# Feed-forward activations of a decoder layer in one tile for the whole stage, with the 2x2 blocks turned

## Chip, cores and metric

One core of a Trainium2 chip (trn2) runs the whole layer in one launch. The metric is device time in microseconds, the time of the slowest core (here the only one), lower is better.

## What is computed

One post-norm decoder layer on 512 tokens of width 2048, in float32. Most of the reference does not matter here. The change lies in the feed-forward part, of which the first matrix product is this:

```python
x = layer_norm(DEEPNORM_ALPHA * x + mix, ln_mix_g, ln_mix_b)
f = jnp.square(jax.nn.relu(x @ w_ff1)) @ w_ff2        # w_ff1: 2048 x 8192, w_ff2: 8192 x 2048
x = layer_norm(DEEPNORM_ALPHA * x + f, ln_ff_g, ln_ff_b)
```

## The kernel before

**Precision.** Every float32 product is made of three matmuls: each operand is split into a high part (written by ScalarE, `wh`, `aH`, L87) and a rest (written by VectorE, `wl`, `aL`, L88), and high x high, high x rest and rest x high are added in PSUM.

**The first feed-forward product in units.** The 8192 hidden columns are taken as 16 groups of 512. Group 0 is computed plainly. Groups 1 to 15 are the units (`FUnit`). A unit is a 2x2 block product (tokens in two halves of 256, features in two halves of 1024, hidden columns in two halves of 256) made with seven products M1 to M7 instead of eight, in the order M1, M5, M6, M3, M7, M2, M4 (`ORDER`). Each product is two pieces (`FPiece`), so a unit is pieces 0 to 13, each 24 matmuls of 256 columns at L654. Its blocks are called by two digits, as "11" or "21". The activations `yH`, `yL` and their sums `ysH`, `ysL` stay on chip. The four weight blocks of a unit (`w1`, 1 MB each, tags handed from unit to unit) are loaded by SyncE's queue at L611: `give` at pieces 6, 7, 9 and 11 of a unit loads the next unit's blocks, in the order "11", "12", "22", "21", each into the buffer of a block that is used up.

**The order of the work is the program's own.** Ahead of piece i, `fill` issues the splits of piece i+2 (ScalarE, then VectorE; M1 and M5 pieces also add one weight block to another on VectorE, L615: for M1, "12" is added onto "11"), then `beside` issues the side work of piece i, then `mult` issues the matmuls of piece i. Three pairs of `wh`, `wl` buffers exist, so a split waits until the matmuls three pieces earlier are done. Every engine takes its instructions in program order. Counting on over the end of a unit, this text calls the next unit's pieces 0, 1, 2 and 3 also pieces 14, 15, 16 and 17.

**The results of a unit.** They are put into `R[g]`, a tile `hpR` of 2 halves x 8 slots x 256 tokens with one buffer (tag "R"). Slots 0 to 3 are the four output blocks. At piece 10 VectorE writes slot 2 (-M1-M6 as copied, less M5) and slot 3 (the copied -M5 less the bank of M1, L663), ScalarE applies the ReLU to both at piece 11 (L666), VectorE writes slot 0 at piece 12, ScalarE applies its ReLU at piece 13. Products M6, M7 and M4 are added in PSUM onto the bank of M1, and M4 is pieces 12 and 13: its first matmul can start only when slot 3's subtraction has read that bank. When the unit is over (`done`, in the next unit's piece 0), ScalarE writes slot 1 with the ReLU of the bank (L620) and squares slots 0 to 3 (L621).

**Sending them out.** In the next unit, for groups 0 to 13, VectorE forms slots 4 to 7 out of slots 0 to 3 at pieces 2 and 3 (`h_sums`, L548). At pieces 5 and 7 slots 1 to 7 of one half are split (`hpH`, L87 and L88) and sent to `h_parts` in DRAM by two transfers of 896 KB each on GpSimd's queue (L555). Slot 0 is not sent: the second product has no factor that is this block alone. Groups 14 and 15 send slots 0 to 3 instead (`h_rest`).

**Other work in the same stage.** On GpSimd's queue, `y_load` at piece 7 brings three 256 KB pieces, and `y_rows` at piece 11 makes two VectorE operations (L526, L527) and sends 256 KB (L531). After the 15 units the second product starts (L789), whose operands come back from `h_parts`.

```python
def h_rows(g):
    R[g] = L2["p"].tile([P, 2, 8, 256], F32, name="hpR", tag="R")
...
elif j == 10:
    h_rows(u.g)
    block(2, u2, v["M5"], OP.subtract)
    block(3, m5, v["M1"], OP.subtract)
```

A new tile on a tag with one buffer may be written when all that used the old tile is done. Inside one tile an instruction waits for the earlier ones whose data it overlaps.

Of the kernel before, what the change touches and what calls it, by code (L numbers as in the profile page):

```python
# [9 lines left out]
F32 = mybir.dt.float32  # L10
F32R = mybir.dt.float32r
I32 = mybir.dt.int32
AF = mybir.ActivationFunctionType
OP = mybir.AluOpType
PSUM = bass.MemoryType.PSUM

P = 128
# [51 lines left out]
def decoder_layer(ctx: ExitStack, tc: tile.TileContext, x, xt, positions, w_in, w_pool, pool_scale,  # L69
                  w_branch_attn, w_branch_pool, w_out, ln_mix_g, ln_mix_b, w_ff1, w_ff2,  # L70
                  ln_ff_g, ln_ff_b, consts, vectors, out, h_parts, h_rest, y_norm, y_parts):
    nc = tc.nc
# [13 lines left out]
    def split(dst_h, dst_l, src):  # L86
        nc.scalar.activation(dst_h, src, AF.Copy)  # L87
        nc.vector.tensor_tensor(dst_l, src, dst_h.bitcast(F32), op=OP.subtract)  # L88
# [348 lines left out]
    L2 = {}  # L437
# [16 lines left out]
    yH, yL = mH, mL  # L454
# [8 lines left out]


    yr, sums = {}, {}
    RAW = {"11": "t11", "12": "t10", "21": "t1", "22": "t12"}
    SUM = {"P1": ("t7", "t8"), "P2": ("t9", "t12"), "P4": ("t11", "t6")}

    def ln1_t(t0, j):
        half, k0 = t0 // 2, 2 * j % 8  # L470
        who = str(half + 1) + str(j // 4 + 1)
        if k0 == 0:
            yr[who] = L2["p"].tile([P, 8, 256], F32, name="yr", tag=RAW[who])
        p = PS.tile([P, 2, 2 * P], F32, name="sc" if j % 2 else "tp", bufs=1)
        for e in range(2):
            k = 2 * j + e
            for t in range(2):
                nc.tensor.transpose(p[:, e, t * P:(t + 1) * P], acc[t0 + t][:, k * P:(k + 1) * P], ident)
        y = yr[who][:, k0:k0 + 2]
        for e in range(2):  # L480
            k = 2 * j + e
            nc.scalar.activation(y[:, e], p[:, e], AF.Identity, bias=bcol[:, k:k + 1], scale=gcol[:, k:k + 1])
        c = slice(2 * j % 4, 2 * j % 4 + 2)
        t = slice(t0 * P, (t0 + 2) * P)
        split(yH[j // 2][:, c, t], yL[j // 2][:, c, t], y)

    def ln1_side(t0):
        return [lambda: ln1_norm(t0)] + [lambda j=j: ln1_t(t0, j) for j in range(8)]
# [4 lines left out]
    def y_sum(name, src):  # L493
        h = L2["p"].tile([P, 8, 256], F32R, name="ysH", tag=SUM[name][0])
        l = L2["p"].tile([P, 8, 256], F32R, name="ysL", tag=SUM[name][1])
        if name == "P2":
            nc.scalar.activation(h, yr[src], AF.Copy, scale=-1.0)
            nc.vector.scalar_tensor_tensor(l, yr[src], -1.0, h.bitcast(F32), op0=OP.mult, op1=OP.subtract)
        else:
            split(h, l, yr[src])  # L500
        sums[name] = (h, l)
# [8 lines left out]
    def y_p3():  # L510

        for c in range(2):
            split(yH[c][:, :, 256:], yL[c][:, :, 256:], yr["21"][:, 4 * c:4 * c + 4])


    def y_load(t, n):
        c = slice(n * 512, (n + 1) * 512)
        nc.gpsimd.dma_start(low["u"][:, 1], y_norm[t, :, c])
        nc.gpsimd.dma_start(low["g"][:, 0], bcast(ln_mix_g, c))
        nc.gpsimd.dma_start(low["g"][:, 1], bcast(ln_mix_b, c))  # L520

    def y_rows(t, n):
        c = slice(n * 512, (n + 1) * 512)
        v, g, b = low["u"][:, 1], low["g"][:, 0], low["g"][:, 1]
        stt = nc.vector.scalar_tensor_tensor
        stt(v, v, ALPHA, g, op0=OP.mult, op1=OP.mult)  # L526
        stt(v, b, ALPHA, v, op0=OP.mult, op1=OP.add)  # L527
        if t >= 2 and n % 2:
            nc.gpsimd.dma_start(g, y_parts[t - 2, :, c])
            return lambda: y_rest(t, c)  # L530
        nc.gpsimd.dma_start(y_parts[t, :, c], v)  # L531
# [11 lines left out]
    R = {}  # L543
# [25 lines left out]
        return {2: lambda: h_sums(g, slice(0, 2)), 3: lambda: h_sums(g, slice(2, 4)),  # L569
                5: lambda: h_parts_out(g, 0), 7: lambda: h_parts_out(g, 1)}  # L570

    def h_rows(g):
        R[g] = L2["p"].tile([P, 2, 8, 256], F32, name="hpR", tag="R")

    def ff1_evac(g):

        def f(b, p):
            if g not in R:
                h_rows(g)
            t = R[g][:, b % 2, 2 * (b // 2):2 * (b // 2) + 2]  # L580
            nc.scalar.activation(t, p, AF.Relu)
            nc.scalar.activation(t, t, AF.Square)
        return f
# [8 lines left out]
    def yblock(who, k):  # L592

        if who in sums:
            return tuple(v[:, k] for v in sums[who])
        if who == "P3":
            who = "21"
        c, t = 2 * (int(who[1]) - 1) + k // 4, slice(256 * (int(who[0]) - 1), 256 * int(who[0]))
        return yH[c][:, k % 4, t], yL[c][:, k % 4, t]

    class FUnit:
# [5 lines left out]

        def get(self, role):
            self.b[role] = L2["p"].tile([P, 8, 256], F32, name="w1", tag=self.tag[role])
            k, c0 = int(role[0]) - 1, self.g * 512 + (int(role[1]) - 1) * 256  # L610
            nc.sync.dma_start(self.b[role], w_ff1[k * 1024:(k + 1) * 1024, c0:c0 + 256].rearrange("(a p) n -> p a n", p=P))  # L611

        def sum(self, role, other, half):
# [3 lines left out]
        def done(self):  # L617

            if self.ps:
                nc.scalar.activation(R[self.g][:, :, 1], self.ps["M1"].rearrange("p (n t) -> p n t", n=2), AF.Relu)  # L620
                nc.scalar.activation(R[self.g][:, :, :4], R[self.g][:, :, :4], AF.Square)  # L621

        def give(self, role, new):
# [32 lines left out]
    def beside(u, j, last):  # L656

        v = {m: p.rearrange("p (n t) -> p n t", n=2) for m, p in u.ps.items()}
        m1, m5, u2 = low["m"][:, 0], low["m"][:, 1], low["u"][:, 0]
        act = nc.scalar.activation  # L660

        def block(slot, in0, in1, op):
            nc.vector.tensor_tensor(R[u.g][:, :, slot], in0.rearrange("p (n t) -> p n t", n=2), in1, op=op)  # L663

        def relu(a, b):
            act(R[u.g][:, :, a:b], R[u.g][:, :, a:b], AF.Relu)  # L666

        if j == 0:
            last.done()
        elif j == 2:  # L670
            act(m1, u.ps["M1"], AF.Copy)
        elif j == 4:
            act(m5, u.ps["M5"], AF.Copy, scale=-1.0)
            u.sum("12", "22", 0)
        elif j == 6:
            act(u2, u.ps["M1"], AF.Copy, scale=-1.0)
            u.sum("12", "22", 1)
            u.give("22", u.order[0])
        elif j == 7:
            u.give("12", u.order[1])  # L680
            if chunks:
                y_load(*chunks[0])
        elif j == 8:
            u.sum("11", "21", 0)
        elif j == 9:
            u.sum("11", "21", 1)
            u.give("21", u.order[2])
        elif j == 10:
            h_rows(u.g)
            block(2, u2, v["M5"], OP.subtract)  # L690
            block(3, m5, v["M1"], OP.subtract)
        elif j == 11:
            u.give("11", u.order[3])
            relu(2, 4)
            if chunks:
                u.rest = y_rows(*chunks.pop(0))
        elif j == 12:
            block(0, m1, v["M2"], OP.add)
        elif j == 13:
            relu(0, 1)  # L700
        if j == 3 and last.rest:
            last.rest()
        if j in last.out:
            last.out[j]()


    MO = (("11", 1), ("21", 3), ("22", 7), ("11", 4), ("E", 6), ("22", 5), ("21", 2))
    HOP = ("t7", "t8", "t9", "t12", "t11", "t6", "R")
    hop, part, PS2 = {}, {}, [None]
    seeded = {1: (2, 0), 2: (2, 512), 6: (0, 0), 3: (0, 512)}  # L710

    def h_load(c, m):
        v = L2["p"].tile([P, 2, 4, 256], F32R, name="hop", tag=HOP[m])
        for e in range(2):
            nc.gpsimd.dma_start(v[:, e], h_parts[c, e, MO[m][1] - 1])
        hop[m] = v
# [86 lines left out]
    def bcast(v, c=slice(0, DM)):  # L803
        return bass.AP(tensor=v.tensor, offset=v.offset + c.start, ap=[[0, P], [1, c.stop - c.start]])

    def tail_load(m):
        if m < 4:
            rest[m] = L2["p"].tile([P, 2, 4, 256], F32R, name="hop", tag=HOP[m])
            for e in range(2):
                nc.gpsimd.dma_start(rest[m][:, e], h_rest[e, :, m])  # L810
        elif m < 6:
            rest[m] = L2["p"].tile([P, DM], F32, name="ln", tag=HOP[m])
            nc.gpsimd.dma_start(rest[m], bcast(ln_ff_g if m == 4 else ln_ff_b))
# [37 lines left out]
    def block(t, n):  # L851

        return rows[n // 2, t // 2][:, t % 2, n % 2]
# [38 lines left out]
    funits = [FUnit(g) for g in range(1, 16)]  # L892
# [5 lines left out]
    for a, b in zip(funits, funits[1:] + units[:1]):  # L898
        a.next = b
        a.order = ("11", "12", "22", "21") if b is not units[0] else ("11", "21", "22", "12")  # L900
    funits[0].tag = {"11": "t0", "12": "t2", "22": "t3", "21": "t1"}
    units[0].tag = {"E": "t10"}
    fpieces = [FPiece(u, j) for u in funits for j in range(14)]
    pieces = [Piece(u, j) for u in units for j in range(14)]
# [21 lines left out]
    p = PS.tile([P, 512], F32, name="mm", bufs=6)  # L926
# [105 lines left out]
    for n in range(2):  # L1032
# [10 lines left out]
        for T in range(2):  # L1043
            v = rows[0, T][:, :, n]
# [52 lines left out]
```

## Time and profile before

| | us |
|---|---|
| median of 3 runs | 2547.76 (2546.31 to 2551.65) |
| the profiled execution | 2548.12 |
| its span in the profile | 2546.3 |
| stage of the 15 units | about 1173 to 1914 of the span |

The span is what the engines' records cover; the profiled execution has 1.8 us around it. In the rows below, a timeline row is: start in us from the span's start, duration in us, engine, line, operation, out<-in, how many, and in brackets the engine's idle time before it and what ended it. A row of waits is: who waited <- for whom, us in total, times, longest.

### The profile page before, as it was taken

The numbers are of one execution on the slowest core, as the hardware profiler recorded it, in microseconds if no ns is written. First come the engines' busy times: TensorE is split into PE (matmuls) and PEld (weight loads), VectorE is DVE, ScalarE is ACT, GpSimd is POOL, SyncE is SP. The second block draws the span as 40 slices with busy tenths as digits, with TensorE's granted clock in tenths as the row PEclk, the third lists the DMA queues.
The fourth block names the chain that finished last, engine by engine and source line by source line (L and its number), as shares of the span: only waits on it lengthen the run. The fifth ranks groups of instructions, "written<-read, shape, count | busy, mean of one in ns | idle before, by whom it ended". The sixth has DMA issues, their size and how long they took to land.

```text
span 2546.3 us, 31612 instructions
## 1 busy us (share of the span) xinstructions
PE 2421.3 (95%) x13096; PEld 2106.9 (83%) x13096; DVE 1591.8 (63%) x1641; ACT 963.0 (38%) x1030; POOL 168.8 (7%) x256
## 2 busy tenths in 40 slices
PE   9999999999999999998788888878989999999998
PEld 7888888877788888888788888878888888888886
DVE  4522254655433243468677677767767888888886
ACT  4323212344322232265345444444445433343330
POOL 0000000000000000010111110101111001100000
PEclk9999999999999999999899989989999999999999
DMA  6323323222233333464655664565478575655642
GB/s 200 91 91 107 105 93 98 83 84 76 79 95 99 100 110 114 149 227 148 217 177 169 207 195 141 189 212 163 164 262 290 204 245 198 231 191 175 228 166 99
DMA packets 201919, 399.32 MB, mean 157 GB/s; under 512 B 11312, under 2 KB 73904, under 8 KB 201008
## 3 DMA queue, kind: packets, MB, share of 16 engines
q1 hardware_dynamic: 163312, 257.83, 31.3%
q0 software_dynamic: 36160, 135.28, 15.8%
q10 hardware_dynamic: 2304, 4.20, 0.5%
q8 instruction: 102, 1.67, 0.3%
q14 instruction: 41, 0.34, 0.0%
HBM read 329.11 MB, written 68.16 MB: 156 GB/s over the span
## 4 chain that ended last, share of the span: by engine, by line
PE 81%; DMA 8%; DVE 4%; issue 4%; ACT 2%; POOL 0%; POOLq 0%; SPq 0%; DVEq 0%; ACTq 0%
PE mm L147 41%; PE pp L789 21%; PE mm L654 13%; DMA h_parts<-hpR 7%; PE pp L834 3%; DVE hpR L88 1%; DVE wl L88 1%; ACT hpH L87 1%; ACT wh L87 1%; PE sc L351 1%; PE tp L383 1%; DVE w L615 1%; DMA h_parts<-hpH 0%; DMA wr<-in_w_out 0%; DVE hpR L663 0%
## 5 line engine op out<-in xcount | busy, mean ns | idle before, releaser
L87 ACT ACTIVATE wh<-w 128x1024 fp32r<-128x1024 f32 x406 | 429.6, 1059 | 566.3 <-PE pp L789 296.5
L88 DVE TENSOR_TENSOR wl<-wr,wh 128x1024 fp32r<-128x1024 f32 (+1 forms) x228 | 277.4, 1219 | 568.6 <-ACT wh L87 567.8
L88 DVE TENSOR_TENSOR wl<-w,wh 128x1024 fp32r<-128x1024 f32 x406 | 494.3, 1220 | 130.5 <-ACT wh L87 130.3
L789 PE MATMUL pp<-wh,hop 128*128 128x512 f32 x1568 | 483.0, 389 | 0.7 <-ACT hpR L620 0.7
L87 ACT ACTIVATE wh<-wr 128x1024 fp32r<-128x1024 f32 (+1 forms) x228 | 240.4, 1055 | 613.1 <-PE mm L147 565.2
L147 PE MATMUL mm<-aH,wh 128*128 128x512 f32 (+1 forms) x1024 | 396.5, 387 | 0.6 <-ACT wh L87 0.6
L147 PE MATMUL mm<-aH,wl 128*128 128x512 f32 (+1 forms) x1024 | 387.2, 378 | 5.1 <-DVE wl L88 5.1
L147 PE MATMUL mm<-aL,wh 128*128 128x512 f32 (+1 forms) x1024 | 386.5, 377 | 0.0
L654 PE MATMUL mm<-aH,wh 128*128 128x256 f32 x960 | 287.1, 299 | 100.8 <-DVE hpR L663 100.8
L789 PEld LDWEIGHTS pp<-wh,hop 128*128 128x128 f32 x1568 | 294.3, 188 | 61.9 <-ACT hpR L620 0.9
L789 PE MATMUL pp<-wl,hop 128*128 128x512 f32 x784 | 305.2, 389 | 0.1
L654 PE MATMUL mm<-aH,wl 128*128 128x256 f32 x960 | 283.9, 296 | 2.4 <-DVE wl L88 2.4
L654 PE MATMUL mm<-aL,wh 128*128 128x256 f32 x960 | 284.5, 296 | 0.0
L654 PEld LDWEIGHTS mm<-aH,wh 128*128 128x128 f32 x960 | 198.4, 207 | 103.2 <-issue 103.2
L147 PEld LDWEIGHTS mm<-aH,wl 128*128 128x128 f32 x1024 | 193.8, 189 | 41.5 <-DVE wl L88 6.2
L147 PEld LDWEIGHTS mm<-aH,wh 128*128 128x128 f32 x1024 | 193.9, 189 | 38.9 <-ACT wh L87 2.2
L147 PEld LDWEIGHTS mm<-aL,wh 128*128 128x128 f32 x1024 | 194.0, 189 | 37.1 <-issue 1.9
L654 PE MATMUL mm<-ysH,wl 128*128 128x256 f32 x720 | 204.0, 283 | 2.3 <-DVE wl L88 2.3
L654 PE MATMUL mm<-ysH,wh 128*128 128x256 f32 x720 | 203.8, 283 | 0.0
L654 PE MATMUL mm<-ysL,wh 128*128 128x256 f32 x720 | 203.7, 283 | 0.0
L654 PEld LDWEIGHTS mm<-aH,wl 128*128 128x128 f32 x960 | 197.5, 206 | 2.8 <-DVE wl L88 2.8
L654 PEld LDWEIGHTS mm<-aL,wh 128*128 128x128 f32 x960 | 198.4, 207 | 0.0
(174 smaller groups left out, 3357.3 us busy)
## 6 DMA issues: line engine op xcount, KB each, us to landing
wr<-in_w_in SPq DMA_DIRECT2D x127, 512.0 KB, 3.6
w<-in_w_ff SPq DMA_DIRECT2D x60, 1024.0 KB, 14.6
w<-in_w_ff SPq DMA_DIRECT2D x112, 512.0 KB, 6.4
hop<-h_parts POOLq DMA_DIRECT2D x98, 512.0 KB, 7.1
h_parts<-hpH POOLq DMA_DIRECT2D x28, 896.0 KB, 9.1
h_parts<-hpR POOLq DMA_DIRECT2D x28, 896.0 KB, 9.6
wr<-in_w_out SPq DMA_DIRECT2D x40, 512.0 KB, 3.6
wr<-in_w_ff SPq DMA_DIRECT2D x32, 512.0 KB, 3.7
```

Of the source, the lines that this page charges most:

```text
L87: nc.scalar.activation(dst_h, src, AF.Copy)
L88: nc.vector.tensor_tensor(dst_l, src, dst_h.bitcast(F32), op=OP.subtract)
L147: nc.tensor.matmul(o, l, r, start=first and j == 0, stop=last and j == 2)
L351: nc.tensor.matmul(p[:, :n], qT[h][:, qb * P:(qb + 1) * P], kT[h][:, :n], start=True, stop=True)
L383: nc.tensor.matmul(p[:, k * P:], vt["v"][:, k, h * HD:(h + 1) * HD], pT[h][:, k, k * P:], start=k == 0, stop=k == 3)
L615: nc.vector.tensor_tensor(self.b[role][:, c], self.b[role][:, c], self.b[other][:, c], op=OP.add)
L654: nc.tensor.matmul(o, l, r, start=first, stop=self.j % 2 == 1 and k == 3 and i == 2, skip_group_check=True)
L789: nc.tensor.matmul(u.ps[:, t], l, r, start=q + j == 0, stop=q == 3 and j == 2)
L834: nc.tensor.matmul(o, l, r, start=first and i == 0, stop=last and i == 2)
```

## The change

One `hpR` tile is made once, by group 0, and all groups use it. The token halves and the hidden-column halves are exchanged between the block names, so that the block subtracted from the bank of M1 at piece 10 is the one of slot 0. The block that was written beside it moves to piece 12 (slot 1), the one of piece 12 to piece 13 (slot 3). The ReLU of slots 0 and 1 comes at piece 13, that of slot 3 in `done` ahead of that of slot 2 (from PSUM). The ReLU at piece 11 is gone. The tags of two activation buffers ("t1" and "t11") change places with the names.

```diff
-    RAW = {"11": "t11", "12": "t10", "21": "t1", "22": "t12"}
-    SUM = {"P1": ("t7", "t8"), "P2": ("t9", "t12"), "P4": ("t11", "t6")}
+    RAW = {"11": "t1", "12": "t10", "21": "t11", "22": "t12"}
+    SUM = {"P1": ("t7", "t8"), "P2": ("t9", "t12"), "P4": ("t1", "t6")}
...
-        who = str(half + 1) + str(j // 4 + 1)
+        who = str(2 - half) + str(j // 4 + 1)
...
-            split(yH[c][:, :, 256:], yL[c][:, :, 256:], yr["21"][:, 4 * c:4 * c + 4])
+            split(yH[c][:, :, :256], yL[c][:, :, :256], yr["21"][:, 4 * c:4 * c + 4])
...
-    def h_rows(g):
-        R[g] = L2["p"].tile([P, 2, 8, 256], F32, name="hpR", tag="R")
-
     def ff1_evac(g):
 
         def f(b, p):
-            if g not in R:
-                h_rows(g)
+            if not R:
+                R.update(dict.fromkeys(range(16), L2["p"].tile([P, 2, 8, 256], F32, name="hpR", tag="R")))
...
-        c, t = 2 * (int(who[1]) - 1) + k // 4, slice(256 * (int(who[0]) - 1), 256 * int(who[0]))
+        c, t = 2 * (int(who[1]) - 1) + k // 4, slice(256 * (2 - int(who[0])), 256 * (3 - int(who[0])))
...
-            k, c0 = int(role[0]) - 1, self.g * 512 + (int(role[1]) - 1) * 256
+            k, c0 = int(role[0]) - 1, self.g * 512 + (2 - int(role[1])) * 256
...
             if self.ps:
-                nc.scalar.activation(R[self.g][:, :, 1], self.ps["M1"].rearrange("p (n t) -> p n t", n=2), AF.Relu)
+                nc.scalar.activation(R[self.g][:, :, 3], R[self.g][:, :, 3], AF.Relu)
+                nc.scalar.activation(R[self.g][:, :, 2], self.ps["M1"].rearrange("p (n t) -> p n t", n=2), AF.Relu)
                 nc.scalar.activation(R[self.g][:, :, :4], R[self.g][:, :, :4], AF.Square)
...
         elif j == 10:
-            h_rows(u.g)
-            block(2, u2, v["M5"], OP.subtract)
-            block(3, m5, v["M1"], OP.subtract)
+            block(0, m5, v["M1"], OP.subtract)
         elif j == 11:
             u.give("11", u.order[3])
-            relu(2, 4)
             if chunks:
                 u.rest = y_rows(*chunks.pop(0))
         elif j == 12:
-            block(0, m1, v["M2"], OP.add)
+            block(1, u2, v["M5"], OP.subtract)
         elif j == 13:
-            relu(0, 1)
+            block(3, m1, v["M2"], OP.add)
+            relu(0, 2)
...
-    HOP = ("t7", "t8", "t9", "t12", "t11", "t6", "R")
+    HOP = ("t7", "t8", "t9", "t12", "t1", "t6", "R")
...
-    funits[0].tag = {"11": "t0", "12": "t2", "22": "t3", "21": "t1"}
+    funits[0].tag = {"11": "t0", "12": "t2", "22": "t3", "21": "t11"}
```

## Rows read from the trace of the kernel before

**Rows 1.** The page: busy time and share of the span of TensorE.

```profile
PE 2421.3 (95%) x13096; PEld 2106.9 (83%) x13096; DVE 1591.8 (63%) x1641; ACT 963.0 (38%) x1030; POOL 168.8 (7%) x256
```

**Rows 2.** The page: the chain that ended last, by line.

```profile
PE mm L147 41%; PE pp L789 21%; PE mm L654 13%; DMA h_parts<-hpR 7%; PE pp L834 3%; DVE hpR L88 1%; DVE wl L88 1%; ACT hpH L87 1%; ACT wh L87 1%; PE sc L351 1%; PE tp L383 1%; DVE w L615 1%; DMA h_parts<-hpH 0%; DMA wr<-in_w_out 0%; DVE hpR L663 0%
```

**Rows 3.** The waits of the whole span.

```profile
ACT hpR L666 <- DVE hpR L663: 124.0, 14, 10.1
DVE hpR L663 <- DMA h_parts<-hpR: 115.4, 14, 9.1
...
PE mm L654 <- DVE hpR L663: 100.8, 14, 8.4
```

**Rows 4.** TensorE's timeline: the first and the third such wait.

```profile
1219.67 0.55 PE L654 MATMUL mm<-aH,wh 128*128 128x256 f32 x1 [8.44 <-DVE hpR L663]
...
1320.80 0.55 PE L654 MATMUL mm<-aH,wh 128*128 128x256 f32 x1 [6.88 <-DVE hpR L663]
```

**Rows 5.** VectorE's timeline: the first and the last wait of L663.

```profile
1218.24 1.28 DVE L663 TENSOR_TENSOR hpR<-low,mm 128x512 f32<-128x512 f32 x2 [8.84 <-DMA h_parts<-hpR]
...
1863.27 1.28 DVE L663 TENSOR_TENSOR hpR<-low,mm 128x512 f32<-128x512 f32 x2 [8.00 <-DMA h_parts<-hpR]
```

**Rows 6.** TensorE's timeline behind that third wait: neighbours early and late.

```profile
1321.58 0.41 PE L654 MATMUL mm<-aH,wh 128*128 128x256 f32 x1
1321.80 0.41 PE L654 MATMUL mm<-aL,wh 128*128 128x256 f32 x1
...
1324.82 0.28 PE L654 MATMUL mm<-aL,wh 128*128 128x256 f32 x1
1324.94 0.28 PE L654 MATMUL mm<-aH,wl 128*128 128x256 f32 x1
```

**Rows 7.** One unit's stretch: length, busy PE, PEld, DVE, ACT, POOL, clock, DMA share, GB/s.

```profile
1278.60:1327.40 48.80, 41.92 (x336) 41.75 (x335) 36.10 (x35) 23.12 (x23) 8.31 (x12) 0.93 0.64 204
```

**Rows 8.** First unit: L514's split into one token half of aH, aL; TensorE reading.

```profile
1179.22 1.99 ACT L87 ACTIVATE aH<-yr 128x1024 fp32r<-128x1024 f32 x2
...
1181.75 2.35 DVE L88 TENSOR_TENSOR aL<-yr,aH 128x1024 fp32r<-128x1024 f32 x2
...
1177.00 0.28 PE L654 MATMUL mm<-aL,wh 128*128 128x256 f32 x1
```

**Rows 9.** DMA issues at 1301.04, 1303.72 and 1306.38: KB, us to landing.

```profile
w<-in_w_ff SPq DMA_DIRECT2D x1, 1024.0 KB, 17.4
...
w<-in_w_ff SPq DMA_DIRECT2D x1, 1024.0 KB, 17.6
...
h_parts<-hpR POOLq DMA_DIRECT2D x1, 896.0 KB, 13.0
```

**Rows 10.** VectorE's timeline in the second and third unit: five kinds of its work.

```profile
1257.87 1.22 DVE L88 TENSOR_TENSOR wl<-w,wh 128x1024 fp32r<-128x1024 f32 x1
1259.00 1.22 DVE L615 TENSOR_TENSOR w<-w,w 128x1024 f32<-128x1024 f32 x1
...
1275.32 0.68 DVE L663 TENSOR_TENSOR hpR<-low,mm 128x512 f32<-128x512 f32 x1
...
1287.36 1.41 DVE L548 TENSOR_TENSOR hpR<-hpR 128x512 f32<-128x512 f32 x2
...
1296.70 2.02 DVE L88 TENSOR_TENSOR hpR<-hpR,hpH 128x1792 f32<-128x1792 f32 x1
```

**Rows 11.** ScalarE's timeline at the third unit's end: ReLU, square, next split.

```profile
1329.41 0.58 ACT L620 ACTIVATE hpR<-mm 128x512 f32<-128x512 f32 x1
1330.02 1.92 ACT L621 ACTIVATE hpR<-hpR 128x2048 f32<-128x2048 f32 x1
1331.84 1.04 ACT L87 ACTIVATE wh<-w 128x1024 fp32r<-128x1024 f32 x1
```

**Rows 12.** A short wait of TensorE in the first unit; that stretch's clock (columns: rows 7).

```profile
1185.29 0.39 PE L654 MATMUL mm<-ysH,wl 128*128 128x256 f32 x1 [1.54 <-DVE wl L88]
...
1174.00:1190.00 16.00, 12.25 (x98) 11.62 (x97) 14.38 (x13) 12.07 (x17) 0.00 (x0) 1.00 0.21 66
```

## The prediction

> **What bounds the kernel now.** I began with the page. TensorE is busy for 95% of the span [rows 1], so time can be won only where it is kept waiting, or where its clock is down. The chain that ended last shows one place: beside the matmul lines it holds a transfer, h_parts<-hpR, with 7% of the span [rows 2]. The waits say what hangs on it: in 14 places VectorE's L663 waits for that transfer, 115.4 us in all, and TensorE waits 100.8 us for that L663, also 14 times [rows 3]; 14 is the number of units in which an earlier group's results are being sent. I then took the third unit as the pattern; its idle time of 6.88 us [rows 4] is near the mean of 100.8 / 14 = 7.2.
>
> The mechanism: at piece 10 VectorE wants to write into a new `hpR` tile, must wait until both halves of the old one are sent, and keeps behind it the subtraction that reads the bank of M1. TensorE's piece 12 adds onto that bank and stands still.
>
> From the first such wait of L663 to the last are 13 units, (1863.27 - 1218.24) / 13 = 49.6 us each [rows 5]. Matmuls at full speed follow each other after 0.12 us [rows 6] (the last two), so a unit of 14 x 24 of them needs 40.3 us, and a piece 2.88. The excess is 9.3 us: 7.2 of idle time, and 2.1 for matmuls behind it that follow each other after 0.21 to 0.22 us [rows 6] (the first two): after the idle stretch TensorE runs at its 1.2 GHz level for some us (the unit's mean granted clock is 0.93 [rows 7]). 14 x 9.3 = 130 us is what could be had at most.
>
> **The first eviction.** Slot 0 is not sent out. With one tile, the subtraction at piece 10 writes slot 0 while the transfers read slots 1 to 7 of each half. Does it wait all the same, since the slots lie interleaved? A row bears on it: in the first unit L514's split writes one token half of `aH` and `aL`, strided in the same way, and is issued ahead of piece 0's matmuls, which read the other half; those of pieces 0 and 1 were still running at 1177.00, before the split began at 1179.22 (ScalarE) and 1181.75 (VectorE) [rows 8]. They did not wait. So I take it that slot 0's writer doesn't wait, and TensorE's idle 7.2 us and the slow 2.1 us go. Earlier work in slot 0 (the sums, the square) is over by piece 4.
>
> **The other evictions.** Slot 1's writer at piece 12 still waits for both halves' transfers, slot 3's follows at piece 13. Nobody on TensorE reads them, but behind slot 1's on VectorE stand the rest splits of piece 15 and after, and on ScalarE the ReLU at piece 13. I count from the moment when piece 12 could start, 1320.80 - 6.88 = 1313.92 in the third unit. The last transfer was issued at 1306.38 and took 13.0 us [rows 9]: it lands at +5.5. VectorE reaches slot 1 only after the work that the next paragraph prices, at +8.6. So this wait is hidden as long as the transfer is less than 3 us later.
>
> **What the old wait was hiding.** The weight blocks for the next unit. "11" was issued at 1301.04 and took 17.4 us, "12" at 1303.72 and 17.6 us [rows 9]: they land at +4.5 and +7.4. Before, pieces 14 and 15 came behind the wait and found them there. Now piece 14's split needs "11", and the addition of "12" onto "11" stands ahead of slot 1 and of piece 15's split on VectorE. These loads run beside the sending, on the same DMA engines, which were at a share of 0.64 over the unit [rows 7]; nothing in the change moves the three issues against each other, so I keep their durations.
> By the Trainium skill (DMA: Bandwidth & Descriptors, section Queues, rings and completion order) each DMA engine takes turns between the queues that have work. By an even turn at the unit's own rate while busy (204 / 0.64 = 319 GB/s [rows 7]) "11" would be there after 1.05 MB / 160 GB/s = 6.6 us and "12" 6.6 us later, at +0.3; the measured 17.4 and 17.6 us do not bear this out, and the sum goes by the measured ones.
>
> **The sum for a unit.** VectorE's splits and additions take 1.22 us each, and start 1.13 us apart when they follow at once; a block 0.68, two slot sums 1.41, a send split 2.02 [rows 10]. ScalarE's split takes 1.04, L620 0.58, the square 1.92 [rows 11]. A piece needs its rest split at its third matmul, 0.24 us after its start.
> - Piece 14: "11" at +4.5, split to +5.6, rest to +6.8; wanted at 2 x 2.88 + 0.24 = +6.0. TensorE waits 0.8.
> - Piece 15: "12" at +7.4, addition to +8.6, slot 1 to +9.2, rest split to +10.4; wanted at 8.9 + 0.8 = +9.7. It waits 0.7.
> - Piece 16: addition, slot 3 (done at +12.1), rest split to +13.3; wanted at +13.3. No wait.
> - Piece 17: `done` has one operation more. ReLU of slot 3 after +12.1, ReLU of slot 2 and the square, 0.58 + 0.58 + 1.92, to +15.2; only then piece 17's split to +16.2 and rest to +17.4; wanted at 14.6 + 1.5 = +16.1. It waits 1.3.
> Together 2.8 us. VectorE, busy for 36.1 us of the unit [rows 7], reaches the addition at piece 6 that releases "11" about 0.5 us later against piece 12 than now, so I take 3.1 us of waits: 43.4 us a unit, 6.2 less than 49.6.
>
> **Small parts, at nothing.** Of the load at piece 11 ("21", 1 MB) and `y_rows` with its 256 KB, which no longer queue behind the wait on SyncE's and GpSimd's queues, the first runs behind "22" and is wanted only for piece 8's addition; the second adds 256 KB behind the sending, 0.8 us at 319 GB/s, at worst onto "12". The exchange of names moves no work: the same tags are taken and freed by the same steps. After the last unit the second product must wait for L620, which now stands behind one more ReLU: 0 to 0.6 us once, taken as 0.6.
>
> **Sum.** 14 x 6.2 = 87 us, less 0.6: 2548.1 - 86 = 2462 in terms of the profiled execution, which lies 0.4 above the median; **2461 us** predicted. With waits of 1.4 to 5.5 us a unit instead of 3.1 (a load that lands 2 us earlier or 2.5 later), the gain is 14 x 7.9 = 111 to 14 x 3.8 = 53: **2437 to 2495** is the likeliest case's own range.
>
> **Rivals.**
> - *Everything is hidden.* If the weights come early enough, all 9.3 us go: 2548 - 130 = 2418. For it: TensorE has no other wait of note in these units, and an even turn of the queues (the page named above) would give it. Against it: 17.4 and 17.6 us [rows 9], and `done` on ScalarE alone leaves some wait at piece 17.
> - *The burst gets longer.* The load at piece 11 and the 256 KB, 1.3 MB in all, now fall among the others: at 319 GB/s 4 us. If "12" and the sending bear all of it, the unit is 47.4 us, 14 x 2.2 = 31 us are won: 2517. Against it: "21" is issued last on its queue.
> - *The change does not do what it says*: slot 0's writer waits for the transfers although they touch other slots. Then the idle time stays at piece 12: about 2548. Rows 8 speak against it.
> - *Slower: the short waits hold TensorE's clock down.* Instead of one idle stretch there are three short ones within 12 us. If the clock falls to 1.2 GHz in them, each matmul costs 0.09 us more; the 9.3 us are given back after 9.3 / 0.09 = 103 matmuls, a bit more than 4 pieces. If it stays down over pieces 14 to 19, 144 matmuls, the unit is 40.3 + 13.4 = 53.7 us, 4.1 more than now, and the kernel 2605. Against it: in the first unit TensorE was idle in pieces for 16.00 - 12.25 = 3.75 us of 16, one wait of them 1.54 us, and the granted clock stayed at 1.00 [rows 12]. The Trainium skill (TensorE: Matmul & The Clock Gate, section A second HAM failure mode: psum-queue depth-cycling) has a kernel whose frequent short idles between groups of matmuls made its clock swing; rows 12 don't show this.
>
> **How the numbers follow.** Forecast 0.70, everything hidden 0.12, longer burst 0.10, no change 0.04, slower 0.04. The range takes the forecast's own, most of the first rival and a part of the second: 2422 to 2508. About 0.2%, 5 us, is what a measurement of this kernel can tell from no change: faster 0.92, same 0.04, slower 0.04.
>
> **What would show it.** Right: TensorE's wait for L663 is gone; the units are 43 to 44 us apart; VectorE's additions L615 and ScalarE's splits wait for w<-in_w_ff; TensorE has short waits for `wl` at pieces 14, 15 and 17; the granted clock in the stage is near 1.00. Wrong: L663 still waits long for h_parts<-hpR; 1.2 GHz stretches after short waits; units of 40.3 us (the weights were in time) or above 47 (the burst grew).

## The result and the profile after

| | before | after |
|---|---|---|
| median of the runs | 2547.05 us (2546.31 to 2551.65) | 2490.97 us (2488.42 to 2494.17) |
| profiled execution, its span | 2548.12, 2546.3 | 2494.17, 2492.4 |

The ratio is 0.9777, with a 95% interval of 0.976 to 0.9794: 56 us less. 2461 had been forecast, with 2437 to 2495 for the likeliest case and 2422 to 2508 for the range.

The page after, TensorE's busy time (against [rows 1]) and the chain that ended last by line (against [rows 2]); L652 is what was L654, L661 what was L663, L612 what was L615:

```profile
PE 2418.1 (97%) x13096; PEld 2101.9 (84%) x13096; DVE 1585.7 (64%) x1641; ACT 960.9 (39%) x1030; POOL 168.7 (7%) x256
...
PE mm L147 42%; PE pp L785 21%; DMA w<-in_w_ff 10%; PE mm L652 5%; DVE wl L88 4%; PE pp L830 3%; DVE w L612 1%; ACT wh L87 1%; DVE hpR L88 1%; DVE hpR L548 1%; PE sc L351 1%; PE tp L383 1%; DMA part<-y_parts 1%; DVE hpR L661 1%; DMA wr<-in_w_out 0%
```

The transfer of the results (h_parts<-hpR, 7% before) has left the chain; the load of the weights (w<-in_w_ff) has come in with 10%. The waits of the whole span say the same (against [rows 3]):

```profile
ACT hpR L664 <- DVE hpR L661: 83.7, 14, 7.7
...
ACT wh L87 <- DMA w<-in_w_ff: 63.9, 13, 6.5
...
DVE w L612 <- DMA w<-in_w_ff: 53.3, 14, 5.6
PE mm L652 <- DVE wl L88: 52.6, 20, 4.7
```

No wait of L661 for a transfer is left. VectorE's addition L612 waits for the weights in 14 places, and TensorE waits 52.6 us for rest splits, where it had waited 100.8 us for L663. Three of the 20 waits, 4.7 us, lie at the start of the first unit, where there were such waits before [rows 12]; the other 47.9 us are 3.4 a unit, in 12 of the 14 units one single wait.

TensorE's timeline in the third unit (against [rows 4]), then its clock around that wait (columns: stretch, its length, TensorE's busy time, granted clock, DMA share, GB/s):

```profile
1319.11 0.58 PE L652 MATMUL mm<-aH,wl 128*128 128x256 f32 x1 [3.31 <-DVE wl L88]
```

```profile
1317.00:1319.00 2.00, 0.00 (x0) 1.00 0.93 292
1319.00:1321.00 2.00, 1.89 (x9) 0.53 0.22 70
1321.00:1323.00 2.00, 2.00 (x13) 0.62 0.01 4
1323.00:1325.00 2.00, 2.00 (x19) 1.00 0.00 0
```

There is one wait, at the third matmul of piece 15, and behind it TensorE runs at its 1.2 GHz level for some us (granted clock 0.53 and 0.62 in the two stretches that hold it), as it had behind the old wait. The distance of units, from VectorE's timeline of the third block of a unit (against [rows 5]):

```profile
1226.03 0.68 DVE L661 TENSOR_TENSOR hpR<-low,mm 128x512 f32<-128x512 f32 x1
...
1821.13 0.68 DVE L661 TENSOR_TENSOR hpR<-low,mm 128x512 f32<-128x512 f32 x1
```

(1821.13 - 1226.03) / 13 = 45.8 us, where it was 49.6 and 43.4 had been forecast. 40.3 are matmuls at full speed, 3.4 the wait, and the remaining 2.1 the slow matmuls behind it.

The chain that ended last, in order of time, at the end of the third unit shows who sets this:

```profile
1297.31 18.70 DMA w<-in_w_ff
...
1317.24 0.68 DVE hpR L661
1317.92 1.15 DVE wl L88
...
1320.95 0.63 ACT hpR L617
...
1323.91 1.05 ACT wh L87
...
1342.34 19.24 DMA w<-in_w_ff
```

Weight block "12", issued at 1297.31, lands at 1316.01; VectorE adds it, writes slot 1, makes piece 15's rest split; TensorE goes on at 1319.11. And VectorE's timeline shows what follows up to the next landing:

```profile
1316.10 1.22 DVE L612 TENSOR_TENSOR w<-w,w 128x1024 f32<-128x1024 f32 x1 [3.49 <-DMA w<-in_w_ff]
...
1324.98 1.23 DVE L88 TENSOR_TENSOR wl<-w,wh 128x1024 fp32r<-128x1024 f32 x1 [1.68 <-ACT wh L87]
...
1341.09 1.23 DVE L88 TENSOR_TENSOR wl<-w,wh 128x1024 fp32r<-128x1024 f32 x1 [1.21 <-ACT wh L87]
...
1361.67 1.23 DVE L612 TENSOR_TENSOR w<-w,w 128x1024 f32<-128x1024 f32 x1 [3.36 <-DMA w<-in_w_ff]
```

From 1316.01 VectorE has a backlog and works with two pauses (1.68 and 1.21 us) until the rest split that ends at 1342.32. Both pauses are waits for a split on ScalarE, the first behind `done` (ReLUs, square) and the split after it, where the chain runs over ScalarE for 4.0 us from 1320.95. The rest split that ends at 1342.32 was the last use of the old block "12", and the load of the next one is issued at 1342.34. Its issue and the one before, 1297.31, by the DMA issues of those stretches (columns: KB, us to landing):

```profile
w<-in_w_ff SPq DMA_DIRECT2D x1, 1024.0 KB, 18.7
```

```profile
w<-in_w_ff SPq DMA_DIRECT2D x1, 1024.0 KB, 19.2
```

So there is a ring: landing, 26.3 us of work on VectorE and, in between, ScalarE, issue, 19.2 us until the next landing at 1361.58. 26.3 + 19.2 = 45.5 us, near the mean distance of the units. Over the stage the way from landing to issue takes 26.3 us in eight of the 13 intervals, 26.9 in three, in which VectorE has one side operation more (L535), and 27.7 in the first two, in which it has two more (L526, L527); the load takes 17.9 to 20.4, in the mean 19.1. In some stretches the chain runs through TensorE's matmuls instead, but L612's 14 waits for the weights are one a unit. This is the theory that the experiments had to test. Its rivals: VectorE's work as a whole sets the units; or TensorE's own account does (matmuls, its wait, its slow stretch), so that the clock would give its 2 us back if it were held up.

### The profile page after: what moved, and what is told of

It reads as the page before. It is cut to its first block, busy times and chain, and to the rows that moved or that the text cites. A ratio compares the mean times of both kernels' runs of the same rounds, so it can differ in the third digit from the quotient of the medians.

```text
span 2492.4 us, 31596 instructions
## 1 busy us (share of the span) xinstructions
PE 2418.1 (97%) x13096; PEld 2101.9 (84%) x13096; DVE 1585.7 (64%) x1641; ACT 960.9 (39%) x1030; POOL 168.7 (7%) x256
## 3 DMA queue, kind: packets, MB, share of 16 engines
q0 software_dynamic: 36160, 135.28, 16.1%
## 4 chain that ended last, share of the span: by engine, by line
PE 75%; DMA 11%; DVE 8%; issue 3%; ACT 2%; POOLq 0%; SPq 0%; DVEq 0%; ACTq 0%
PE mm L147 42%; PE pp L785 21%; DMA w<-in_w_ff 10%; PE mm L652 5%; DVE wl L88 4%; PE pp L830 3%; DVE w L612 1%; ACT wh L87 1%; DVE hpR L88 1%; DVE hpR L548 1%; PE sc L351 1%; PE tp L383 1%; DMA part<-y_parts 1%; DVE hpR L661 1%; DMA wr<-in_w_out 0%
## 5 line engine op out<-in xcount | busy, mean ns | idle before, releaser
L652 PE MATMUL mm<-aH,wl 128*128 128x256 f32 x960 | 285.9, 298 | 49.7 <-DVE wl L88 49.5
L652 PE MATMUL mm<-aH,wh 128*128 128x256 f32 x960 | 282.3, 294 | 0.0
L652 PE MATMUL mm<-aL,wh 128*128 128x256 f32 x960 | 281.8, 294 | 0.0
L652 PEld LDWEIGHTS mm<-aH,wl 128*128 128x128 f32 x960 | 195.7, 204 | 53.9 <-DVE wl L88 53.6
L652 PE MATMUL mm<-ysH,wl 128*128 128x256 f32 x720 | 204.5, 284 | 3.0 <-DVE wl L88 3.0
L652 PE MATMUL mm<-ysH,wh 128*128 128x256 f32 x720 | 204.5, 284 | 0.0
L652 PE MATMUL mm<-ysL,wh 128*128 128x256 f32 x720 | 204.2, 284 | 0.0
L652 PEld LDWEIGHTS mm<-aH,wh 128*128 128x128 f32 x960 | 195.4, 204 | 0.2 <-ACT wh L87 0.2
L652 PEld LDWEIGHTS mm<-aL,wh 128*128 128x128 f32 x960 | 195.3, 203 | 0.0
```

The source lines that it names most:

```text
L652: nc.tensor.matmul(o, l, r, start=first, stop=self.j % 2 == 1 and k == 3 and i == 2, skip_group_check=True)
```

## Experiments

Ratios are to the kernel before, run on the same chip. They are compared with 0.9777 (0.976 to 0.9794) of the changed kernel.

**One part of the change alone.** First only the tile: the kernel before, with one `hpR` for the whole stage and the old order of the evictions.

```diff
-            if g not in R:
-                h_rows(g)
+            if not R:
+                R.update(dict.fromkeys(range(16), L2["p"].tile([P, 2, 8, 256], F32, name="hpR", tag="R")))
...
         elif j == 10:
-            h_rows(u.g)
             block(2, u2, v["M5"], OP.subtract)
```

> One tile for the whole stage, but the old order: slots 2 and 3 are still written at piece 10. Theory (the gain needs a first eviction into a slot that is not sent): VectorE waits at piece 10 as before, about 8 us in 14 places, and the time is that of before, 2547 us within 5. Rival (the new tile in each unit was itself the cause of the wait): the wait shrinks and the time falls towards 2491.

Measured: 2546.31 us, 0.9994 (0.9985 to 1.0004). Then only the order: the changed kernel, with a new tile at piece 10 of each unit.

```diff
         elif j == 10:
+            R[u.g] = L2["p"].tile([P, 2, 8, 256], F32, name="hpR", tag="R")
             block(0, m5, v["M1"], OP.subtract)
```

> The blocks turned and moved, but a new tile in each unit, taken at piece 10. Theory (both parts are needed): the first write into the new tile waits for the transfers out of the old one, TensorE stands at piece 12 as before, 2547 us within 8. Rival (the move of the other evictions by two pieces is what brings the gain): near 2491.

Measured: 2540.67 us, 0.9966 (0.9953 to 0.9979). The waits of both in the stretch from 1230 to 1850, the tile alone first (its L660 and L651 are L663 and L654 of before):

```profile
DVE hpR L660 <- DMA h_parts<-hpR: 96.3, 12, 9.2
...
PE mm L651 <- DVE hpR L660: 83.9, 12, 7.8
```

```profile
DVE hpR L661 <- DMA h_parts<-hpR: 98.4, 12, 9.1
...
PE mm L652 <- DVE hpR L661: 78.2, 12, 7.3
```

Both keep the wait for the transfers, 8 us each time, and TensorE's wait behind it. Each part alone is worth nothing or 9 of the 56 us; the gain needs a first eviction that touches nothing that is being sent, in a tile that may still be in use.

**The burst of transfers made shorter.** The burst is what is on the DMA engines around "12": the sends of two halves, the weight blocks and, at piece 7, three loads of 256 KB for the residual rows. The changed kernel, with these three loads moved to piece 4, before the burst, in the units of groups 4 to 14.

```diff
         elif j == 7:
             u.give("12", u.order[1])
-            if chunks:
+            if chunks and u.g < 4:
                 y_load(*chunks[0])
...
+        if j == 4 and chunks and u.g > 3:
+            y_load(*chunks[0])
         if j in last.out:
             last.out[j]()
```

> The three loads of 256 KB for the residual rows are issued at piece 4 instead of 7, in the stretch in which the DMA engines are idle, in units 4 to 14 or so (13 of the chunks). Theory (what bounds a unit now is the landing of weight block 12 in a burst that shares the DMA engines): 12 lands some 2 us earlier, TensorE's wait of about 3.3 us falls to about 1 us, the clock stays up more often; 2491 falls by 25 to 50 us, to 2441 to 2466. Rival (VectorE, busy for 36 us of a unit, is the bound): within 8 us of 2491.

Measured: 2447.45 us, 0.9598 (0.9582 to 0.9614), 44 us below the changed kernel. VectorE's work is the same as before the edit, so VectorE's total is not the bound. In those 11 units "12" now lands 10.7 to 16.1 us after its issue (13.9 in the mean); in the three units left as they were it still takes 18.0 to 20.2. VectorE's and TensorE's waits from 1230 to 1850:

```profile
DVE w L612 <- DMA w<-in_w_ff: 22.7, 11, 5.4
...
PE mm L652 <- DVE wl L88: 13.1, 8, 4.7
```

13.1 us of TensorE's wait are left; in the changed kernel it is 43.8 us in the same stretch.

**The clock held up.** The changed kernel, with 20 matmuls on resident data into an unused bank ahead of piece 1 of each unit but the first; they are extra work and no part of the result.

```diff
+        if p.j in (1,) and p.u is not funits[0]:
+            d = PS.tile([P, 512], F32, name="sc", bufs=1)
+            for i in range(20):
+                nc.tensor.matmul(d[:, :256], yH[0][:, 0, :P], yH[0][:, 1, :256], start=True, stop=True)
         p.mult()
```

> 20 extra matmuls of 256 columns into a PSUM bank that nobody reads, ahead of piece 1 in each unit, where TensorE waits about 3.3 us for the weights; they need 2.4 us at full clock and nothing waits for them. Theory (the rest of the excess is matmuls at 1.2 GHz behind that wait, about 2 us a unit): the wait is filled, the granted clock stays near 1.00 in the stage, and the time falls by 15 to 28 us, to 2463 to 2476. Rival (the slow stretch is not due to the idle time, or its cost is hidden behind VectorE anyway): no change, or up to 10 us slower where the wait is shorter than the extra work.

Measured: 2495.02 us, 0.9787 (0.9769 to 0.9804): no change. The same 570 us of the stage in the changed kernel, then here (columns as above):

```profile
1230.00:1800.00 570.00, 530.66 (x4221) 0.95 0.62 197
```

```profile
1230.00:1800.00 570.00, 542.89 (x4394) 0.99 0.61 194
```

The clock was held up, 0.99 for 0.95, and nothing came of it. The ring says why. From the chains, two loads of "12" in the changed kernel, then the same two here:

```profile
1388.52 19.43 DMA w<-in_w_ff
...
1434.29 18.12 DMA w<-in_w_ff
```

```profile
1388.73 20.04 DMA w<-in_w_ff
...
1435.12 19.63 DMA w<-in_w_ff
```

From the first landing to the second issue it is 1434.29 - 1388.52 - 19.43 = 26.34 us there and 1435.12 - 1388.73 - 20.04 = 26.35 here; in all 13 intervals the two kernels agree within 0.03 us, whatever the clock. In the changed kernel the slow matmuls lie in the shadow of the ring: TensorE has 45.8 - 40.3 = 5.5 us a unit to spare, and spends them waiting or running slowly. So the account along TensorE, which adds up to 45.8 us, describes the unit and doesn't set it. The prediction of this run failed, and with it the rival that TensorE's account sets the unit.

**VectorE's time inside and outside the ring.** The rest split of one piece of each unit is made twice, with the same values: of piece 5, between the landing of "12" and the next issue, or of piece 13, between issue and landing.

```diff
             split(self.h, self.l, b[FACTORS[self.what][1]][:, 4 * (j % 2):4 * (j % 2) + 4])
+            if j == 5:
+                nc.vector.tensor_tensor(self.l, b[FACTORS[self.what][1]][:, 4 * (j % 2):4 * (j % 2) + 4], self.h.bitcast(F32), op=OP.subtract)
```

> The changed kernel with the rest split of piece 5 of each unit made twice on VectorE (the same values, 1.14 us more), at a place between the landing of block 12 and the release of the next one. Ring theory: each unit gets 1.1 us longer, 14 x 1.14 = 16 us: 2507, between 2500 and 2512. Rival (VectorE has slack, since it waits about 7 us of a unit for the weights): no change, within 5 us of 2491.

> The same doubling for the rest split of piece 13, which VectorE makes while it would soon wait for the weights, between the release and the landing of block 12. Ring theory: nothing, 2491 within 4 us. Rival (any VectorE time counts): 16 us more, 2507.

Measured: piece 5, 2512.02 us, 0.9862 (0.9846 to 0.9877), at the upper end of what was expected, 21 us more than the changed kernel, 1.5 a unit; piece 13, 2488.67 us, 0.977 (0.9755 to 0.9786), nothing. Two loads of "12" with piece 5's split doubled, from the chain:

```profile
1532.40 18.86 DMA w<-in_w_ff
...
1578.87 19.68 DMA w<-in_w_ff
```

From landing to issue it is 1578.87 - 1532.40 - 18.86 = 27.61 us, where the changed kernel has 26.35: the interval is longer by 1.26, a little more than the instruction's 1.14. With piece 13's split doubled the intervals are those of the changed kernel. The same instruction costs its time in one place and nothing in the other, eight pieces later: the ring as drawn.

**The landing brought forward.** The changed kernel, with each weight block loaded in two transfers of 512 KB, so that the addition for piece 14 needs only the first half of "12".

```diff
-            nc.sync.dma_start(self.b[role], w_ff1[k * 1024:(k + 1) * 1024, c0:c0 + 256].rearrange("(a p) n -> p a n", p=P))
+            for e in range(2):
+                nc.sync.dma_start(self.b[role][:, 4 * e:4 * e + 4], w_ff1[k * 1024 + e * 512:k * 1024 + (e + 1) * 512, c0:c0 + 256].rearrange("(a p) n -> p a n", p=P))
```

> The changed kernel with each weight block loaded by two transfers of 512 KB, first half first, so that the addition for piece 14 waits for half of block 12 only. Ring theory (what sets a unit is: landing of block 12, VectorE's work up to the release of the next unit's block 12, its load): the first half lands about 1.5 us before the second, the ring is that much shorter, 14 x 1.5 = 21 us: 2470, between 2462 and 2478. Rival (TensorE's own account of the waits; the wait moves to the second half one piece later): within 8 us of 2491.

Measured: 2459.39 us, 0.9649 (0.9632 to 0.9667), 32 us below the changed kernel, more than expected. VectorE's timeline, third unit:

```profile
1306.19 1.23 DVE L613 TENSOR_TENSOR w<-w,w 128x1024 f32<-128x1024 f32 x1 [2.71 <-DMA w<-in_w_ff]
...
1309.78 1.23 DVE L613 TENSOR_TENSOR w<-w,w 128x1024 f32<-128x1024 f32 x1 [0.62 <-DMA w<-in_w_ff]
```

Both additions wait for their half, 3.6 us apart in this unit; slot 1 and piece 15's rest split get done between them. Over the 14 units the halves land 1.3 to 3.6 us apart, 2.0 in the mean (the expectation had taken 1.5), and the first lands 16.5 us after its issue, 2.6 less than the whole block does, near the gain of 32 / 14 = 2.3 us a unit.

**Put together.** Early row loads and half loads:

> Both the early loads of the residual rows (2447 alone) and the half loads. Ring theory: TensorE's waits that are left there, 13 us in all by its trace, mostly go: 2435, between 2428 and 2442. Rival: the half loads cost more in issues than they bring, 2447 or above.

Measured: 2427.88 us, 0.9529 (0.9512 to 0.9546), at the lower end of what was expected. In the stretch from 1230 to 1800 VectorE waits 6.5 us for weights and TensorE 4.9 for rest splits. On this, and on the early row loads alone, the first half's results sent a piece earlier:

```diff
-                5: lambda: h_parts_out(g, 0), 7: lambda: h_parts_out(g, 1)}
+                4: lambda: h_parts_out(g, 0), 7: lambda: h_parts_out(g, 1)}
```

> Early row loads and half loads (2428 together), and the first half's results split and sent at piece 4 instead of 5. Ring theory: hardly any wait for the weights is left there (6.5 us on VectorE over the stage, 5 us on TensorE), so a burst that starts a piece earlier brings at most 5 us: 2424 to 2431. Rival (the landing of the weights still sets the units): 10 us or more, below 2418. Third case: the row loads now stand behind the send on GpSimd's queue and join the burst again, 2430 to 2440.

> Early row loads with whole loads (2447), and the first half's results split and sent at piece 4 instead of 5. Ring theory: the burst starts up to 2.9 us earlier, so block 12 lands earlier where TensorE still waits for it, 13 us in all: 2436 to 2444. Rival: VectorE's 2 us for the split of the sent half come between landing and release in either place, and the transfers only shift: within 4 us of 2447.

Measured: 2424.21 us, 0.952 (0.9504 to 0.9536), with the half loads; 2434.88 us, 0.9563 (0.9534 to 0.9592), without. Without half loads, where the weights are still waited for, the earlier burst is worth 13 us by the medians (3 to 11 expected) and 9 by the ratios. All four runs lie below all four with early row loads alone, but they spread from 2427.93 to 2443.96, and the intervals of the two ratios just touch. With half loads it is about 4 us, not clear of the intervals. This fits the ring and is no strong test of it. The page and TensorE's 550 us of the stage in the version with all three edits:

```profile
PE 2389.8 (99%) x13096; PEld 2076.7 (86%) x13096; DVE 1586.4 (66%) x1641; ACT 963.9 (40%) x1030; POOL 168.3 (7%) x256
```

```profile
1230.00:1780.00 550.00, 547.49 (x4555) 1.00 0.70 231
```

TensorE is busy for 547.49 of 550 us at full clock, and 4555 matmuls at 0.12 us are 546.6: the units are bound by their matmuls. The DMA engines as a whole were not the bound in the changed kernel either: they were busy for a share of 0.62 there, and 0.70 here. This version is faster than both kernels, by 123 us than before and by 67 than the change.

## Why the prediction was right, and where its size was off

The cause was right: the old wait went, and what is left is the waiting for the weights. The gain was 56 us instead of 86. That 2491 lies inside 2437 to 2495, 4 us from its end, is in part luck: that range allowed for 5.5 us of waits a unit, and 5.5 us over the 40.3 is what came, but 2.1 of them are slow matmuls, which the sum had at nothing. Of the signs named for being right, three did not show: the units are 45.8 us apart instead of 43 to 44, TensorE waits once a unit instead of three times, and the granted clock of the stage is 0.95 instead of near 1.00; 1.2 GHz stretches behind the waits had been named as a sign of being wrong.

- **The first eviction: right.** Slot 0's writer doesn't wait for transfers out of the interleaved slots of the same tile; L661 waits for none. The first two experiments show that this, and not the tile or the order alone, is the gain. The evidence of [rows 8] was weaker than the prediction makes of it: it shows matmuls passing a write to the other half of a tile, not a write passing transfers.
- **The other evictions: right.** Slot 1's writer is reached after its transfers have landed (1313.27 in the third unit, written at 1317.24).
- **What the old wait was hiding: right in kind.** "11" and "12" are waited for, at the places named. The step that kept their durations failed: "12" took 18.7 and 19.2 us instead of 17.6. About half of that is the choice of the third unit as the pattern: over the 14 units "12" took 17.2 to 18.9 us before, in the mean 18.3, and 19.1 after. The step gave as reason that nothing moves the three issues against each other. But "21" and the 256 KB of `y_rows` now go out at 1307.12 and 1308.72, before "12" lands, where they used to go out after it; that was the second rival's mechanism. That these two transfers make the 0.8 us was not tried by itself; that 768 KB less in the burst brings 44 us was.
- **The sum for a unit: the term that failed.** It was made along TensorE, as 2.8 us of waits and 0.3 for VectorE being later at the releasing addition. The waits came out at 3.4 us, in one place instead of three, since VectorE's addition at piece 14 holds up all that follows, and behind one longer wait the clock fell, 2.1 us that I had put at nothing. But the 45.8 us are not made of these: the ring sets them, in the mean 26.7 us from landing to issue and 19.1 of transfer. The sum never asked when the next "12" can be issued. With the old mean transfer the ring gives 26.7 + 18.3 = 45.0: of the 2.4 us that the sum's 43.4 falls short of 45.8, 1.6 are the ring that it did not see, 0.8 the longer transfer.
- **Rivals.** *Everything is hidden*: not for this change, but the version with all three edits comes to 2424, near the 2418 worked out for it. *The burst gets longer*: partly true, as said. *The change does nothing*: fell. *Slower, by the clock*: fell; the clock did drop behind single waits, so the mechanism is there, but the ring leaves room for it, and the run with the clock held up was no faster. (Its own sum was loose: 144 matmuls at 0.09 us more are 13.0 us, not 13.4, and the three waits themselves were left out.) The Trainium skill (TensorE: Matmul & The Clock Gate, section A second HAM failure mode: psum-queue depth-cycling) ties short idles to lost throughput; here the clock's loss had no price, as that run shows.
- **Small parts: right for the end**, where the second product's first wait for the ReLU grew from 0.7 to 1.2 us. Whether "21" and the 256 KB could be put at nothing is open, as said above.

## What to carry to other kernels

When a wait is taken away, look for what used to arrive during it, and make the next sum around the loop that this arrival closes (release of a buffer, transfer, the work up to the next release), not along the busiest engine. An engine with waits and slow stretches may only be filling the time that such a loop leaves it; doubling one instruction inside the loop and one outside tells the two apart. In a burst, move out whatever is not needed by its end, and cut a large load so that its first user needs only the first part.

## What the hardware showed that was not expected

In the changed kernel the clock fell behind 13 of the 14 waits at piece 15, those of 2.40 to 4.75 us (granted clock 0.53 to 0.75 in the 6 us after each), and not in the one unit where the wait came in three parts of 0.76, 1.70 and 0.76 us. The length of a wait alone does not decide it: with the 20 extra matmuls the clock fell behind a wait of 1.74 us (0.72 in the 6 us from 1223.40) and not behind one of 2.10 (1.00 from 1364.88). In the unit with the three parts, the last of TensorE's waits there, and its granted clock in the 14 us around the three (1.00 in each stretch):

```profile
1554.95 0.39 PE L652 MATMUL mm<-ysH,wl 128*128 128x256 f32 x1 [0.76 <-DVE wl L88]
```

```profile
1542.00:1544.00 2.00, 1.24 (x10) 1.00 1.15 252
...
1546.00:1548.00 2.00, 0.30 (x2) 1.00 0.91 292
1548.00:1550.00 2.00, 2.00 (x18) 1.00 0.33 109
...
1554.00:1556.00 2.00, 1.24 (x10) 1.00 0.00 0
```

The load of "12", 1 MB, needed 17.2 to 18.9 us before the change and 17.9 to 20.4 after it; cut into two transfers, its first half landed 2.0 us before the second, in the mean. 768 KB moved out of a burst of 7424 KB (four sends of 896 KB, the 768 KB, three weight blocks) were worth 44 us over the stage, 4 us for each of the 11 units in which they were moved.

From the landing of "12" to the issue of the next, over nine pieces, the interval repeats within a few hundredths of a us from unit to unit, and grows by about the time of every operation that VectorE has more. Such a constant interval, beside a transfer that varies, is how a ring can be seen in a trace.
